# A fused ReLU-gated MLP: the unused branch's DMAs moved to GpSimd, the last pair of output blocks reordered, and its last piece copied out by two engines

## The chip, the cores and the metric

The kernel runs on one core of one Trainium2 chip. The metric is device microseconds (us) of one execution. A timed group of runs lists every execution; most groups here have five or six of the kernel under test and eleven of the kernel before, taken in the same rounds on the same chip. A ratio is the mean time of one kernel's runs over that of the other's in the same rounds, so it is not quite the ratio of the medians that are quoted beside it. (In the experiments the recorded ratios come out, to within 0.0001, when the first run of each kernel, the profiled one, is left out; where means are quoted below, they are of all runs.)

## The reference

```python
def reference(x, w1, w2):                # x 16x256x512, w1 512x4096, w2 2048x512, float32
    h = x @ w1
    gate, value = np.split(h, 2, axis=-1)
    h = np.maximum(gate, 0) * value
    return (h @ w2).astype(np.float32)
```

## The kernel before

The kernel computes both matrix products by a seven-product scheme (products P1 to P7 with precomputed sums of blocks, instead of eight) in 16-bit floats. That is only accurate enough if the data are of ordinary size, so while it works it gathers statistics, and a verdict `unfit` chooses at the end whether a plain "general way" recomputes everything. With these inputs the general way never runs, but all five engines come to that branch at the end of every execution.

```python
    with ExitStack() as fast:
        unfit = fast_way(fast, tc, x2, w1, w2, out2, flag)
    with tc.If(unfit > 0, label="general"):
        with ExitStack() as general:
            general_way(general, tc, x2, w1, w2, out2)     # its DMAs all on nc.sync

# fast_way, second product: a Pair is two 128-row output blocks, made of seven products.
        def P2(self):
            self.o = tmp.tile([P, 2, DO], F32, name="o", tag="tmp")
            nc.scalar.activation(self.o[:, 0, :DO // 2], self.X, COPY, scale=1 / GS)
            if self.end:
                self.send(0, slice(0, DO // 2))            # send: nc.sync.dma_start to the output
        # ... P6 (ScalarE copies Y to pu), P3 and P7 (VectorE: o <- W or Y, + pu; then send) ...
        def P4(self):
            nc.scalar.activation(self.o[:, 1, :DO // 2], self.Y, COPY, scale=1 / GS)
            self.send(1, slice(0, DO // 2 if self.end else DO))

    # order of the products in the last pair (number 3) of the last block of rows:
    LAST_ORDER = ORDER.replace("P5 3, P2 3, P6 3, P3 3, P7 3", "P2 3, P6 3, P5 3, P7 3, P3 3")   # then P4 3
```

TensorE's program is thousands of instructions, fetched while it runs. The kernel starts with 24 warm-up matmuls (`NWARM`) on zeros; some experiments alter those to shift the program by a few instructions.

## Time and profile before

| | before |
|---|---|
| time, median of the first 3 runs | 309.0 us (308.88 to 310.2) |
| span of the profiled execution | 307.5 us |
| TensorE busy, granted clock | 98%, 0.996 |
| last matmul issued, its result ready | 302.66, about 302.93 |
| last store issued by SyncE, landed | 303.38, 305.81 |
| end | 307.46 |

The page of the kernel before; PE is TensorE. The last line is the chain of waits that ended last, by engine.

```profile
span 307.5 us, 5285 instructions
...
PE 300.7 (98%) x1905; PEld 184.0 (60%) x1905; DVE 235.9 (77%) x388; ACT 176.4 (57%) x348; POOL 151.4 (49%) x189
...
PE 96%; DMA 1%; SPq 0%; POOL 0%; ACT 0%; issue 0%
```

TensorE is the bound for 303 us. Nothing in the change touches the number of matmuls, so what is at stake is the tail after 302.93. Its parts are read from the timeline (columns: start us, length us, what) and from the views of single source lines (count: shortest/median/longest ns, first and last start us). First the last copy, and the last store with its time from issue to landing (a store has landed when the semaphore that its shares count up has received the last of them):

```profile
302.97 0.39 ACT L405 ACTIVATE o<-Y 128x256 f32<-128x256 f32 x1 [2.23 <-PE Y L362]
...
L370 SPq DMA_DIRECT2D out_dram<-o x1: 1072/1072/1072, 303.4 to 303.4; - x1
...
DMA to landing us min/median/max: 2.4/2.4/2.4
```

Then the line of the `If` in the kernel before, which each engine's sequencer (marked q) passes, and SyncE's closing waits:

```profile
L42 SPq EVENT_SEMAPHORE  x8: 17/17/17, 305.0 to 305.8; - x8
...
L42 PEldq COMPARE_BRANCH  x1: 496/496/496, 301.8 to 301.8; - x1
L42 DVEq COMPARE_BRANCH  x1: 90/90/90, 302.1 to 302.1; - x1
...
L42 SPq COMPARE_BRANCH  x1: 73/73/73, 304.5 to 304.5; - x1
```

```profile
L785 SPq EVENT_SEMAPHORE  x11: 28/28/28, 305.9 to 306.5; - x11
L785 SPq DRAIN  x2: 7/10/13, 306.6 to 306.6; - x2
```

Two things stand out. SyncE has eight bookkeeping waits on the not-taken side of the `If`; the eighth waits for the last store to land (305.81), and only then come eleven more closing waits: 1.65 us from landing to the end of the span. And the issue of the last store took 1.07 us where 0.33 is usual.

DMA records of that stretch (303 to 306 us) also show queues that carry no data of the kernel, but instructions:

```profile
q1 hardware_dynamic: 298, 0.27, 27.7%
q8 instruction: 1, 0.02, 2.1%
q14 instruction: 2, 0.02, 1.9%
```

### The profile page before, as it was taken

The numbers are of one execution on the slowest core, as the hardware profiler recorded it, in microseconds if no ns is written. First come the engines' busy times: TensorE is split into PE (matmuls) and PEld (weight loads), VectorE is DVE, ScalarE is ACT, GpSimd is POOL, SyncE is SP. The second block draws the span as 40 slices with busy tenths as digits, with TensorE's granted clock in tenths as the row PEclk, the third lists the DMA queues.
The fourth block names the chain that finished last, engine by engine and source line by source line (L and its number), as shares of the span: only waits on it lengthen the run. The fifth ranks groups of instructions, "written<-read, shape, count | busy, mean of one in ns | idle before, by whom it ended". The sixth has DMA issues, their size and how long they took to land.

```text
span 307.5 us, 5285 instructions
## 1 busy us (share of the span) xinstructions
PE 300.7 (98%) x1905; PEld 184.0 (60%) x1905; DVE 235.9 (77%) x388; ACT 176.4 (57%) x348; POOL 151.4 (49%) x189
## 2 busy tenths in 40 slices
PE   7999999999999999999999999999999999999994
PEld 6844444588844444478864444458884444448883
DVE  2579888899768888887438888889536888888841
ACT  2488886455865555538845555546865555553231
POOL 2389999800069899200029889700007998700000
PEclk9999999999999999999999999999999999999998
DMA  6976779964765260001354910000335110001132
GB/s 207 357 257 190 227 177 174 225 123 87 270 193 86 69 136 3 0 0 67 136 175 103 207 34 2 0 2 24 115 108 167 35 34 0 3 1 34 53 120 74
DMA packets 35837, 32.88 MB, mean 107 GB/s; under 512 B 14432, under 2 KB 31328, under 8 KB 35680
## 3 DMA queue, kind: packets, MB, share of 16 engines
q1 hardware_dynamic: 33536, 26.22, 28.0%
q0 software_dynamic: 2272, 6.29, 11.4%
q8 instruction: 16, 0.26, 0.4%
q14 instruction: 13, 0.11, 0.1%
HBM read 27.26 MB, written 12.58 MB: 130 GB/s over the span
## 4 chain that ended last, share of the span: by engine, by line
PE 96%; DMA 1%; SPq 0%; POOL 0%; ACT 0%; issue 0%
PE Y L250 26%; PE X L250 17%; PE W L250 17%; PE Y L362 14%; PE X L362 9%; PE W L362 9%; DMA w_stage<-in_w_dram 1%; PE X L325 1%; PE W L325 1%; PE Y L325 1%; PE Y L498 0%; PE X L498 0%; SPq L488 0%; PE Y L154 0%; POOL w_B L466 0%; ACT o L405 0%
## 5 line engine op out<-in xcount | busy, mean ns | idle before, releaser
L250 PEld LDWEIGHTS <-w_T 128*128 128x128 f16 x496 | 48.3, 98 | 57.3 <-POOL w_T L232 1.1
L179 POOL TENSOR_TENSOR fold<-xh 128x1024 f32<-128x1024 f16 x16 | 30.3, 1894 | 94.5 <-DMA xh<-x 93.7
L250 PE MATMUL X<-x_A,w_B 128*128 128x512 f16 x248 | 73.8, 379 | 0.0
L250 PE MATMUL Y<-x_S,w_T 128*128 128x512 f16 x220 | 65.5, 379 | 0.0
L250 PEld LDWEIGHTS <-w_B 128*128 128x128 f16 x372 | 36.4, 98 | 42.0
L277 DVE SCALAR_TENSOR_TENSOR cc<-W,pu 128x512 f32<-128x512 f32 x62 | 42.9, 691 | 21.2 <-ACT pu L271 20.4
L257 ACT COPY Y<-X 128x512 f32<-128x512 f32 x62 | 35.4, 571 | 38.2 <-PE X L250 37.9
L271 ACT ACTIVATE pu<-Y 128x512 f32<-128x512 f32 x62 | 37.1, 598 | 33.9 <-PE Y L250 32.9
L182 POOL TENSOR_TENSOR fold<-fold 128x512 f32<-128x512 f32 (+2 forms) x96 | 51.8, 539 | 7.5
L362 PEld LDWEIGHTS <-w_stage 128*128 128x128 f16 x512 | 50.0, 98 | 5.8
L287 DVE SCALAR_TENSOR_TENSOR cc<-Y,pu 128x512 f32<-128x512 f32 x62 | 42.9, 691 | 6.7
L282 DVE SCALAR_TENSOR_TENSOR g<-X,cc 128x512 f16<-128x512 f32 x62 | 42.8, 691 | 2.3
L299 DVE SCALAR_TENSOR_TENSOR g<-Y,cc 128x512 f16<-128x512 f32 x62 | 42.2, 681 | 1.8 <-PE Y L250 1.8
L362 PEld LDWEIGHTS <-g 128*128 128x128 f16 x384 | 37.6, 98 | 8.2
L264 ACT ACTIVATE pu<-W 128x512 f32<-128x512 f32 x62 | 37.2, 600 | 0.8 <-PE W L250 0.6
L250 PE MATMUL W<-x_S,w_B 128*128 128x512 f16 x124 | 36.9, 379 | 0.0
L250 PE MATMUL W<-x_S,w_T 128*128 128x512 f16 x124 | 36.9, 379 | 0.0
L250 PE MATMUL Y<-x_A,w_T 128*128 128x512 f16 x124 | 36.9, 379 | 0.0
L362 PE MATMUL X<-w,g 128*128 128x256 f16 x256 | 31.9, 273 | 0.0
L394 DVE SCALAR_TENSOR_TENSOR o<-W,pu 128x256 f32<-128x256 f32 x16 | 6.8, 422 | 19.8 <-PE W L362 19.8
L169 DVE TENSOR_TENSOR w_stage<-g 128x1024 f16<-128x1024 f16 x32 | 21.4, 683 | 0.2
L232 POOL TENSOR_TENSOR w_T<-w_stage 128x512 f16<-128x512 f32 (+1 forms) x16 | 18.7, 1177 | 2.5 <-DMA w_stage<-in_w_dram 2.5
(100 smaller groups left out, 306.2 us busy)
## 6 DMA issues: line engine op xcount, KB each, us to landing
w_stage<-in_w_dram SPq DMA_DIRECT2D x14, 512.0 KB, 6.2
out_dram<-o SPq DMA_DIRECT2D x26, 256.0 KB, 2.1
x<-in_x_dram POOLq DMA_DIRECT2D x4, 1024.0 KB, 9.0
xh<-x SPq DMA_DIRECT2D x16, 256.0 KB, 3.0
w<-in_w_dram POOLq DMA_DIRECT2D x2, 1024.0 KB, 10.2
out_dram<-o SPq DMA_DIRECT2D x12, 128.0 KB, 1.7
w_stage<-in_w_dram SPq DMA_DIRECT2D x4, 256.0 KB, 5.4
x_S<-in_x_dram SPq DMA_DIRECT2D x4, 256.0 KB, 6.1
```

The costliest lines, as they stand in the source:

```text
L169: eng.tensor_tensor(o[n], o[i0], o[i1], op=op)
L179: nc.gpsimd.tensor_tensor(fold, t, t, op=MULT)
L182: nc.gpsimd.tensor_tensor(fold[:, :, :m], fold[:, :, :m], fold[:, :, m:2 * m], op=ADD)
L250: nc.tensor.matmul(ps, wop[wn][:, b, self.jb * P:(self.jb + 1) * P], self.xo[xn][:, b, :], start=fresh and b == 0, stop=b == 1, skip_group ...
L257: nc.scalar.copy(out=self.Y, in_=self.X)
L264: nc.scalar.activation(self.p5, self.W, COPY, scale=GS)
L271: nc.scalar.activation(self.u2, self.Y, COPY, scale=GS)
L277: nc.vector.scalar_tensor_tensor(out=self.c12, in0=self.W, scalar=GS, in1=self.u2, op0=MULT, op1=ADD)
L282: nc.vector.scalar_tensor_tensor(out=self.g[:, self.jb, :TH], in0=self.X, scalar=0.0, in1=self.c12, op0=MAX, op1=MULT)
L287: nc.vector.scalar_tensor_tensor(out=self.c22, in0=self.Y, scalar=GS, in1=self.p5, op0=MULT, op1=ADD)
L299: nc.vector.scalar_tensor_tensor(out=self.g[:, self.jb, TH:], in0=self.Y, scalar=0.0, in1=self.c22, op0=MAX, op1=MULT)
L362: nc.tensor.matmul(ps, self.op[an][:, i], vop[wn][:, i], start=name in ("P1", "P5") and i == 0, stop=i == NJ // 2 - 1, skip_group_check=True)
```

## The change

The intent: take SyncE's bookkeeping off the end by letting GpSimd, idle since 290 us, own the general way's DMAs; let the stores of the last pair leave as early as possible; and halve the last copy by giving it to two engines.

```diff
 # general_way: all four dma_start calls (two for weights, one for x, one for the output)
-            nc.sync.dma_start(...)
+            nc.gpsimd.dma_start(...)
 # class Pair
+        def outputs(self):                     # makes self.o if P2 or P7 is the first to need it
+            if self.o is None:
+                self.o = tmp.tile([P, 2, DO], F32, name="o", tag="tmp")
         def P4(self):
-            nc.scalar.activation(self.o[:, 1, :DO // 2], self.Y, COPY, scale=1 / GS)
+            split = DO // 4 if self.end and self.t == NB // 2 - 1 else DO // 2
+            nc.scalar.activation(self.o[:, 1, :split], self.Y[:, :split], COPY, scale=1 / GS)
+            if split < DO // 2:
+                nc.vector.tensor_scalar(out=self.o[:, 1, split:DO // 2], in0=self.Y[:, split:],
+                                        scalar1=1 / GS, scalar2=None, op0=MULT)
             self.send(1, slice(0, DO // 2 if self.end else DO))
-    LAST_ORDER = ORDER.replace("P5 3, P2 3, P6 3, P3 3, P7 3", "P2 3, P6 3, P5 3, P7 3, P3 3")
+    LAST_ORDER = ORDER.replace("P5 3, P2 3, P6 3, P3 3, P7 3", "P6 3, P5 3, P7 3, P2 3, P3 3")
```

Below, the three parts are called *GpSimd DMAs*, *order* and *split*.

More of the change, by code (lines that the diff above doesn't have):

```diff
@@ L62, in general_way @@
             t = xp.tile([P, 1024], F32, name="g_t", tag="g_t")
-            nc.sync.dma_start(out=t, in_=w1[k * P:(k + 1) * P, j:j + 1024])
+            nc.gpsimd.dma_start(out=t, in_=w1[k * P:(k + 1) * P, j:j + 1024])
             nc.vector.tensor_copy(out=w1_sb[:, k, j:j + 1024], in_=t)
@@ L66, in general_way @@
         t = xp.tile([P, DO], F32, name="g_t", tag="g_t")
-        nc.sync.dma_start(out=t, in_=w2[h * P:(h + 1) * P, :])
+        nc.gpsimd.dma_start(out=t, in_=w2[h * P:(h + 1) * P, :])
         nc.vector.tensor_copy(out=w2_sb[:, h], in_=t)
@@ L72, in general_way @@
             t = xp.tile([P, D], F32, name="g_t", tag="g_t")
-            nc.sync.dma_start(out=t, in_=x2[c * TH + b * P:c * TH + (b + 1) * P, :])
+            nc.gpsimd.dma_start(out=t, in_=x2[c * TH + b * P:c * TH + (b + 1) * P, :])
             for k in range(NK):
@@ L93, in general_way @@
             nc.vector.tensor_copy(out=o, in_=p[:, :DO])
-            nc.sync.dma_start(out=out2[c * TH + b * P:c * TH + (b + 1) * P, :], in_=o)
+            nc.gpsimd.dma_start(out=out2[c * TH + b * P:c * TH + (b + 1) * P, :], in_=o)
 def fast_way(ctx, tc, x2, w1, w2, out2, flag):
@@ L344, in __init__ @@
         def __init__(self, s, g, t):
-            self.s, self.t = s, t
+            self.s, self.t, self.o = s, t, None
             self.end = s == NS - 1 and t != NB // 2 - 2
@@ L382, in P2 @@
         def P2(self):
-            self.o = tmp.tile([P, 2, DO], F32, name="o", tag="tmp")
+            self.outputs()
             nc.scalar.activation(self.o[:, 0, :DO // 2], self.X, COPY, scale=1 / GS)
@@ L398, in P7 @@
         def P7(self):
+            self.outputs()
             nc.vector.scalar_tensor_tensor(out=self.o[:, 1, DO // 2:], in0=self.Y, scalar=1 / GS, in1=self.pu[:, 0],
@@ L404, in P4 @@
         def P4(self):
-            nc.scalar.activation(self.o[:, 1, :DO // 2], self.Y, COPY, scale=1 / GS)
+            split = DO // 4 if self.end and self.t == NB // 2 - 1 else DO // 2
+            nc.scalar.activation(self.o[:, 1, :split], self.Y[:, :split], COPY, scale=1 / GS)
+            if split < DO // 2:
+                nc.vector.tensor_scalar(out=self.o[:, 1, split:DO // 2], in0=self.Y[:, split:], scalar1=1 / GS, scalar2=None,
+                                        op0=MULT)
             self.send(1, slice(0, DO // 2 if self.end else DO))
```

## The prediction

> **What bounds the kernel.** The page shows PE busy 98% of 307.5 us, and the chain of waits is 96% PE at a granted clock of 0.996. None of the three edits adds or removes a matmul; the instruction order shows the same 1905 on PE. So only the 4.5 us after the last matmul can change. From the timeline and the per-line views of the last 6 us, that tail runs as follows:
>
> - The last product (P4) starts at 301.89 and its result is ready at about 302.93. ScalarE copies 128x256 from 302.97 for 0.385 us.
> - SyncE issues the last store at 303.38. This issue took 1.07 us where 0.33 is usual. It overlaps a 16 KB fetch of instructions by DMA, 303.06 to 304.07.
> - SyncE's branch is at 304.50, its next instruction at 305.03. There stand eight bookkeeping waits of the `If` (305.03 to 305.83), one per hardware DMA queue semaphore, each of which adds what the general way would have counted. The eighth is passed at 305.83, just after the last store lands (305.81, 2.4 us after its issue).
> - Then 11 closing waits, about 0.062 us each, reach the closing drains at 306.58 and 306.65; 0.81 us of barrier ends at 307.46.
>
> **1. General way's DMAs on GpSimd.** They never run. But the not-taken side of the `If` no longer adjusts the hardware DMA semaphores on SyncE: its eight waits go. GpSimd adjusts the software DMA semaphores instead, at about 289.7, where it branches and then idles to the end. SyncE goes through 12 closing waits, of which the one for the last store is the last. So the other eleven (11 x 0.062 = 0.68 us) run while the store is landing, instead of after it. From landing to the drain: now 0.77 us, then about 0.1. Saves about 0.65 us, all on the critical path. SyncE's jump over the general way's instructions also shortens (ScalarE's, over none, took 0.13 us where SyncE's took 0.46); the Trainium skill ("Runtime: NRT & Kernel Launch", Instruction fetch mechanics) says that a taken branch to a page not held forces a fetch. I expect this to be hidden behind the landing.
>
> **2. Last copy split.** The built program makes VectorE wait for ScalarE's half, not for PE. The Trainium skill ("PSUM — Partial Sum Buffer", PSUM bank collisions raise a hardware error) says two engines must not touch one bank at once, so the halves run in series. Estimates from widths 256 and 512 in this trace: ScalarE 0.28 us, VectorE 0.29, handover 0.05: the store is ready at 303.61 instead of 303.36, 0.25 us later. This loses, unless it hides in the issue's stall: if that still ends near 304.45, landing stays at 305.8; without the stall it lands near 305.5.
>
> **3. Order P6 P5 P7 P2 P3 P4.** P3 and P4 stay last. P7's store leaves 0.87 us earlier, P2's later; neither ends the kernel. P6's operands are ready 0.26 us before it starts. Zero.
>
> **Sum.** 0 (order), 0 to +0.25 (split), -0.65 (waits), 0 to -0.3 (stall or branch): about -0.7 us. Predicted 308.3 us, 8 in 10 within 307.8 to 308.9. Faster by over 2%: 0.01; within: 0.98; slower: 0.01.
>
> **What would show it.** On SyncE, no waits of the `If` line after its branch, 12 closing waits, the last passed at the landing, and the drain about 0.1 us later. VectorE's 128x128 copy starts after ScalarE's ends. PE's end is unchanged at 302.9.
>
> **What would make it wrong.** PE stalling in the new order; the last issue stalled longer, or not at all; SyncE reaching the last wait only after the landing; GpSimd's software-DMA bookkeeping holding it up beyond 305; a run-to-run spread (308.9 to 310.2) as large as the gain.

## The result

309.04 us median (308.64 to 309.22, 6 runs) against 309.47 (308.88 to 310.2, 6 runs): ratio 0.9986, 95% interval 0.9971 to 1.0001. That is within 2%, as forecast, but outside the predicted range of 307.8 to 308.9; the gain is 0.4 us and not 0.7. A second group gave 308.77 against 309.38, ratio 0.9989 (0.9976 to 1.0003).

The profile after, in the same order. The page:

```profile
span 307.4 us, 5284 instructions
...
PE 300.7 (98%) x1905; PEld 184.8 (60%) x1905; DVE 236.9 (77%) x389; ACT 176.2 (57%) x348; POOL 151.2 (49%) x189
```

The last copy, now in two halves, and the last store:

```profile
302.85 0.28 ACT L411 ACTIVATE o<-Y 128x128 f32<-128x128 f32 x1 [1.36 <-PE Y L362]
...
303.15 0.29 DVE L413 TENSOR_SCALAR o<-Y 128x128 f32<-128x128 f32 x1 [0.76 <-ACT o L411]
...
L374 SPq DMA_DIRECT2D out_dram<-o x1: 332/332/332, 303.5 to 303.5; - x1
...
DMA to landing us min/median/max: 3.0/3.0/3.0
```

The line of the `If`, and SyncE's closing waits:

```profile
L42 POOLq EVENT_SEMAPHORE  x5: 17/43/43, 289.8 to 290.2; - x5
...
L42 PEldq COMPARE_BRANCH  x1: 1976/1976/1976, 300.8 to 300.8; - x1
...
L42 DVEq COMPARE_BRANCH  x1: 90/90/90, 303.2 to 303.2; - x1
...
L42 SPq COMPARE_BRANCH  x1: 68/68/68, 303.9 to 303.9; - x1
```

```profile
L794 SPq EVENT_SEMAPHORE  x12: 28/28/28, 304.1 to 306.5; - x12
L794 SPq DRAIN  x2: 7/10/13, 306.6 to 306.6; - x2
```

And the DMA records from 303 to 306.5 us (packets, MB, share of 16 engines' time):

```profile
q1 hardware_dynamic: 288, 0.26, 22.7%
q8 instruction: 1, 0.02, 2.6%
q14 instruction: 1, 0.01, 1.2%
```

The first step of the prediction is there to the letter: SyncE's eight waits at the `If` are gone, GpSimd does the bookkeeping at 290, ten of the twelve closing waits are over by 304.7. Landing to end is now 0.96 us (306.47 to 307.43) instead of 1.65. But SyncE then stands at the last two waits for 1.8 us, because the stores had not landed: the last one 3.0 us after its issue instead of 2.4, and the one before it 3.7 us instead of 2.7. What the bookkeeping gave, the landing took back. And TensorE's branch took 1.98 us where it had taken 0.50.

So the question is what holds up stores of 128 KB that could land in 1.7 us (the store just before these two did, in both kernels).

### The profile page after: what moved, and what is told of

The parts are those of the page before. It is cut to its first block, busy times and chain, and to the rows that moved or that the text cites. A ratio compares the mean times of both kernels' runs of the same rounds, so it can differ in the third digit from the quotient of the medians.

```text
span 307.4 us, 5284 instructions
## 1 busy us (share of the span) xinstructions
PE 300.7 (98%) x1905; PEld 184.8 (60%) x1905; DVE 236.9 (77%) x389; ACT 176.2 (57%) x348; POOL 151.2 (49%) x189
## 4 chain that ended last, share of the span: by engine, by line
PE 96%; DMA 2%; SPq 0%; POOL 0%; issue 0%; DVE 0%; ACT 0%
PE Y L250 26%; PE X L250 17%; PE W L250 17%; PE Y L362 14%; PE X L362 9%; PE W L362 9%; DMA w_stage<-in_w_dram 2%; PE X L325 1%; PE W L325 1%; PE Y L325 1%; PE Y L507 0%; SPq L497 0%; PE X L507 0%; PE Y L154 0%; POOL w_B L475 0%
```

## The theories and the experiments

**Theory A: fetches of instructions.** The q8 records are TensorE's program: each is 16,384 bytes, and from the fifth to the thirteenth, eight fetches, TensorE starts 2,048 instructions in the kernel before, 256 for each fetch. (That q8 is TensorE's is inferred from this count.) One such fetch begins 0.7 to 1.4 us after the end of TensorE's branch in every trace that has the branch. A store is cut into 16 shares (its semaphore is updated 16 times), taken here as one for each DMA engine; a fetch is one record of 0.9 to 1.5 us, taken to lie on one engine. The share of the store that queues behind it should come late, and a store has landed only when its last share has.

The semaphore records of the trace show each share. In the changed kernel, 15 shares of the store before last had landed by 304.12 and the sixteenth at 306.16. Later runs are added here to see whether it is a rule; all times are us in the trace, from the records of instruction packets and semaphore updates:

```
kernel                    TensorE's 16 KB     store before last:        last store:
                          fetch, to           15th share, 16th share    16th share
before                    303.06  304.07      305.04  305.25            305.81 (its issue stalled)
changed                   303.53  304.97      304.12  306.16            306.47
changed, again            303.14  304.34      303.69  305.51            305.82
GpSimd DMAs alone         303.51  304.43      305.00  305.62            305.93
GpSimd DMAs + order       304.13  305.29      305.09  306.48            306.79
GpSimd DMAs + split       302.96  304.39      304.16  305.58            306.14 (its issue stalled)
```

In all six, the sixteenth share of the store before last lands 1.17 to 1.19 us after the end of the fetch, and the last store 0.31 us after that (or, where its issue stalled, 1.74 to 1.75 us after the fetch). Where the fifteenth share is late as well (305.00 to 305.09 in three rows), it comes 0.95 to 1.13 us after the end of an 8 KB fetch on queue 14, of which more below. The Trainium skill ("DMA: Bandwidth & Descriptors", Queues, rings and completion order) says that a DMA engine serves its queues in turn, a packet at a time, and, in its section Why a DMA increments its semaphore by 16 and not by 1, that a DMA's semaphore counts its shares. Both fit. The DMA packet records of GpSimd DMAs + order show the wait itself: after 305.2 only 18 packets of stores are left, one after another. The first starts at 305.27, as the fetch ends (305.29). Eight of 1 KB and one of 4 bytes are the late share of the store before last; the next nine, to 306.34, are the last store's. No record here names the engine, so that it is the same one is still inferred.

**Theory B: the change's own later and closer stores.** The split makes the last store later and the order moves the others; the landing follows. **Chance:** landings of stores scatter.

The first group: one part alone, the split undone, TensorE's branch later, and no branch at all.

**GpSimd DMAs alone** (the changed kernel with the other two parts undone).

```diff
-            split = DO // 4 if self.end and self.t == NB // 2 - 1 else DO // 2
+            split = DO // 2
-    ... "P6 3, P5 3, P7 3, P2 3, P3 3")
+    ... "P2 3, P6 3, P5 3, P7 3, P3 3")
```

> The general way's DMAs on GpSimd alone; old order of the last pair, last piece copied by ScalarE alone. Theory A (the bookkeeping is gone as predicted, but what ends the kernel is the landing of the last two stores, held up by a 16 KB fetch of instructions that falls among them): the drain follows the last landing by about 0.08 us (0.77 before); the last store is issued at 303.3 to 303.4; its landing takes 2.3 to 3.0 us if a 16 KB fetch lies within 1 us of its issue; span 306.6 to 307.2, time 0.2 to 0.7 us under the kernel before. Theory B (the split and the order delay the landing): without them the landing is as in the kernel before, about 2.4 us after the issue at 303.38, so 305.8, span 306.75, time 0.7 us under the kernel before.

Measured: 308.61 us against 309.07, ratio 0.9969 (0.9947 to 0.9992). In the trace the last store, issued at 303.26, landed at 305.93, 2.67 us later; span 306.9. So by the ratios part of the change alone gains more than the whole: 0.31% of 309, nearly 1 us (the intervals overlap; the second group repeats it). The landing is late here too, as A has it, but B's 2.4 us is not far off: this run alone does not separate the two.

**GpSimd DMAs and order, no split.**

```diff
-            split = DO // 4 if self.end and self.t == NB // 2 - 1 else DO // 2
+            split = DO // 2
```

> The changed kernel with its last piece copied by ScalarE alone. Theory A: the last store is issued 0.20 to 0.25 us earlier than in the changed kernel (303.25 instead of 303.47), but the landing still ends with the share of the DMA engine that also fetched instructions, near 306.0 to 306.5; time within 0.3 us of the changed kernel. Theory B (the split costs its 0.25 us in full): landing and time 0.25 us earlier.

Measured: 309.03 against 309.07, ratio 0.9984 (0.9966 to 1.0002), as slow as the changed kernel. Relative to TensorE the store left earlier, but its landing is tied to the fetch (table above). TensorE's branch took 1.94 us. This run differs from the one before by the order alone (means 309.01 and 308.49, not clear of the noise). The 0.25 us that B expected from undoing the split does not show.

**TensorE's branch later, by 8 idle matmuls.**

```diff
             advance(stream, 112, jobs)
+            late = new_w()
+            for _ in range(8):
+                arm(late)          # 512 columns of zeros into a spare buffer
```

> The changed kernel with 8 idle matmuls of 512 columns (8 x 0.216 = 1.7 us) at the end of TensorE's program, so that TensorE branches 1.7 us later and nothing else moves. Theory A: the 16 KB fetch that began at 303.53 begins at about 305.2, after the last store's data has gone; the last two stores land 1.7 to 2.0 us after their issue (all 16 shares by about 305.4); span about 306.4, time 0.8 to 1.1 us under the changed kernel. Theory B, and the theory that the late landing is chance: landing unchanged near 306.2 to 306.5, time unchanged or later.

Measured: 309.04 against 309.07, ratio 0.9991. A miss: the fetch did not move as expected. It began at 304.01, not 305.2, because the branch is taken by the sequencer, which runs well ahead of the matmuls: it came to the branch at 301.77, with all eight idle matmuls and the eight of P4 still to be issued. Still, the store before last now escaped (landed in 1.87 us) and the late share, 306.12, was the last store's, 1.18 us after the end of the fetch (304.94).

**No branch: the `If` and its general way left out** (right for these inputs only).

```diff
-    with tc.If(unfit > 0, label="general"):
-        with ExitStack() as general:
-            general_way(general, tc, x2, w1, w2, out2)
```

> The changed kernel without the If and its general way (right for these inputs; the verdict is computed and loaded but not used): no engine branches at the end. Theory A: no 16 KB fetch within the last 3 us; the last two stores land 1.7 to 2.0 us after their issue; span 306.2 to 306.5, time 0.8 to 1.2 us under the changed kernel. Theory B and chance: landing near 306.2 to 306.5 as in the changed kernel, time within 0.3 us of it.

Measured: 307.86 against 309.07, ratio 0.995 (0.9931 to 0.9968). The last store, and the fetches of the whole execution from the page of this run (16 on q8 in the kernel before and the changed one):

```profile
L371 SPq DMA_DIRECT2D out_dram<-o x1: 332/332/332, 303.5 to 303.5; - x1
...
DMA to landing us min/median/max: 1.7/1.7/1.7
```

```profile
q8 instruction: 15, 0.25, 0.4%
```

Split and order are as in the changed kernel, the store is issued at the same 303.48, and it lands at 305.18 instead of 306.47. B, which would leave the landing where it was, falls as the main cause: it is the branches and what they fetch. All engines' branches went here, so this run does not say whose.

The second group repeats the changed kernel and GpSimd DMAs alone on another chip, adds the remaining pair of parts, and tries again to hold TensorE's branch back, now with many small matmuls.

**The changed kernel again.**

> The changed kernel itself once more, as the standard of this group and to see whether its tail repeats. Theory A (stores held up by the fetches after the branches; a wait of TensorE's branch for the page fetched before it): TensorE's branch again takes about 2 us (0.4 to 0.5 with the old order), its 16 KB fetch ends about 304.9, the store before last lands 1.19 us after that end and the last one another 0.31 us later. Chance: other landings, with no such spacing.

Measured: 308.77 against 309.38, ratio 0.9989. Branch 2.04 us, fetch's end 304.34, landings 1.17 and 1.48 us after it: the tail repeats.

**GpSimd DMAs alone, again.**

> The general way's DMAs on GpSimd alone, once more, on one chip with the changed kernel. Theory A: TensorE's branch takes 0.4 to 0.5 us, its fetch ends about 304.4 and the last store lands 1.5 us later, near 305.9; time 0.3 to 0.6 us under the changed kernel, so the order and the split together cost that. Chance: the same time as the changed kernel within 0.15 us.

Measured: 308.3 against 309.38, ratio 0.9969 (0.9956 to 0.9982), branch 0.50 us. In this trace the whole execution ran 0.7 us later and the last store's issue stalled (0.99 us), so the landing was 1.74 us after the fetch's end. On this chip it is 0.43 us under the changed kernel (means 308.44 and 308.87; 95% of such a difference lies within about 0.5 us, so it is not clear of the noise by itself).

**GpSimd DMAs and split, old order.**

```diff
-    ... "P6 3, P5 3, P7 3, P2 3, P3 3")
+    ... "P2 3, P6 3, P5 3, P7 3, P3 3")
```

> The changed kernel with the old order P2 P6 P5 P7 P3 P4, so DMAs on GpSimd and the split. Theory A, order part: with the old order the TensorE fetch before the branch starts near 298.4 instead of 299.9, the branch takes 0.4 to 0.5 us instead of 2, the fetch after it ends about 304.1 to 304.5; the last landing comes 1.5 us after the later of that end and, for one share, follows VectorE's own 8 KB fetch, which the split moves from 303.5 to 304.4 or later: near 306.0; time 0.2 to 0.5 us under the changed kernel. Rival (the split is what costs, not the order): as slow as the changed kernel.

Measured: 308.56 against 309.38, ratio 0.9977 (0.9964 to 0.999); branch 0.50 us. With the old order the branch took 0.41 to 0.50 us in all four traces so far, with the new one 1.3 to 2.0 us in all four.

**TensorE's branch held back by 44 tiny matmuls** (GpSimd DMAs, old order, no split).

```diff
             advance(stream, 112, jobs)
+            late = new_w()
+            for _ in range(44):
+                nc.tensor.matmul(late[:32, :64], warm_b[:, :32], warm_b[:, :64], start=True, stop=True)
```

> DMAs on GpSimd alone, and 44 tiny matmuls (32 columns of weights, 64 of data) at the end of TensorE's program, so that its sequencer, which runs some 32 instructions ahead, reaches the branch late. Theory A: the branch comes near 304 and its fetch starts after 304.7, when the last store's data has gone: the last store lands 1.7 to 2.0 us after its issue at 303.27, near 305.1 to 305.3; span 306.1 to 306.3, time 0.5 us or more under DMAs on GpSimd alone and the fastest that keeps the general way. If the tiny matmuls take over 0.055 us each, TensorE itself ends after 305.3 and takes part of it back. Chance: no change.

Measured: 308.01 against 309.38, ratio 0.9964 (0.9949 to 0.9979). Its branch, and the landing of its last store:

```profile
L42 PEldq COMPARE_BRANCH  x1: 412/412/412, 303.4 to 303.4; - x1
```

```profile
L374 SPq DMA_DIRECT2D out_dram<-o x1: 332/332/332, 303.1 to 303.1; - x1
...
DMA to landing us min/median/max: 2.0/2.0/2.0
```

The branch came at 303.40, the fetch began at 304.56, and the last store landed 2.0 us after its issue, at 305.13. The tiny matmuls took 0.03 us each and TensorE was done at 304.1, before anyone waited for it. It keeps the general way, and it is faster than both kernels. It is 0.34 us under GpSimd DMAs alone (means 308.10 and 308.44), where 0.5 or more was expected, and that is within the noise. By the spacing, what is left of the delay belongs to the 8 KB fetch on queue 14 (303.36 to 303.68): the store before last landed at 304.83, 1.15 us after its end, and the last one 0.3 us later.

### Why the new order makes the branch long

The built program shows which semaphores TensorE waits for, instruction by instruction. P7 must wait until ScalarE has copied P6's result. In the new order P7 is the third of the last six products, not the fourth, so this wait stands 16 instructions earlier. **Theory D:** the sequencer runs ahead until a wait that is not met. In the old order it ran past the end of a 16 KB page of program before it met that wait, and the next page was asked for early (298.37 in the kernel before). In the new order the wait stands just before the end of the page: the fetch began at 299.90, after ScalarE's copy was done (298.86). TensorE's branch then has to wait for this fetch: in the six traces with the long branch (two of the changed kernel, two of GpSimd DMAs + order, the 8 idle matmuls, and the converse below) it ended 1.44 to 1.46 us after the end of that fetch. And the fetch that follows the branch is later in turn: it began 0.55 to 1.58 us after the start of the last matmul in these six traces, and 0.39 to 0.97 in the four with the old order and its short branch. **Rival E:** the order as such crowds the stores.

The test moves the end of the page without touching the last pair: more or fewer instructions in the warm-up.

**Changed kernel, page's end 20 instructions earlier.**

```diff
-    for i in range(NWARM):
+    for i in range(NWARM - 3):
         nc.tensor.matmul(Y[:, :P], warm_b[:, :P], warm_b[:, :P], start=True, stop=True)
+    for i in range(13):
+        nc.tensor.matmul(Y[:32, :64], warm_b[:, :32], warm_b[:, :64], start=True, stop=True)
```

> The changed kernel with 20 more instructions in TensorE's warm-up (3 of its 24 matmuls replaced by 13 tiny ones, about the same time), so that the point at which the sequencer asks for its next 16 KB of program comes 20 instructions earlier in the last pair: before the wait of P7 for the copy of P6 instead of just after it. Theory D (the new order costs because that wait holds the sequencer short of the page's end, the page comes 1.5 us late and the branch has to wait for it): the fetch before the branch starts near 298.4 instead of 299.9, the branch takes 0.4 to 0.5 us instead of 2 and ends near 301.3, the fetch after it ends at 303.0 to 304.1; VectorE's fetch still falls on the last store; last landing 305.2 to 306.0, time 0.3 to 1.0 us under the changed kernel (308.8). Rival E (the order itself moves the stores together, whatever the pages): branch still 2 us, no gain.

Measured: 309.4 against 309.08, ratio 1.0011 (0.9998 to 1.0024). The branch was short, as D says; the time, expected 0.3 to 1.0 us shorter, went the other way. The fetch, now 302.53 to 303.85, fell on the issue of the store before last, which stalled for 1.33 us; the last store had to wait for SyncE until 304.31; and then VectorE's own fetch (below) fell on both of their shares, and the last landed at 307.01.

**The same without the split.**

```diff
-            split = DO // 4 if self.end and self.t == NB // 2 - 1 else DO // 2
+            split = DO // 2
```

> The same, without the split: DMAs on GpSimd, new order, the page's end before the wait. Theory D: as the one before, and VectorE's fetch starts near 303.5 and ends 303.8: last landing 304.95 to 305.4, span 305.9 to 306.4, time 0.8 to 1.2 us under the kernel with the same order and no split (309.0): the new order is then better than the old, not worse. Rival E: 309.0 as before.

Measured: 308.35 against 309.08, ratio 0.9981 (0.9963 to 0.9999), last landing 305.21. 1.1 us under the run with the split on the same chip (means 308.33 and 309.43). The kernel with the same order, no split and the page's end after the wait had 309.03 in another group: 0.7 us by the medians, where 0.8 to 1.2 was expected. That the new order would then be better than the old does not show (0.9981 against 0.9969 twice).

**The converse: old order, page's end 16 instructions later** (GpSimd DMAs, no split).

```diff
-    for i in range(NWARM):
-        nc.tensor.matmul(Y[:, :P], warm_b[:, :P], warm_b[:, :P], start=True, stop=True)
+    for i in range(NWARM - 8):
+        nc.tensor.matmul(Y[:, :192], warm_b[:, :P], warm_b[:, :192], start=True, stop=True)
```

> The converse: DMAs on GpSimd, old order, no split, and 16 instructions fewer in TensorE's warm-up (16 matmuls of 192 columns for 24 of 128), so that the page's end falls after the same wait in the old order. Theory D: the fetch before the branch starts at 300.6 to 301.2 instead of 298.4, the branch takes 1.4 to 2 us instead of 0.45, the fetch after it ends at 305.0 to 305.8, last landing 306.5 to 307.3, time 0.6 to 1.2 us over the same kernel with the page as it was (308.4). Rival E: 308.4, branch 0.45 us.

Measured: 309.34 against 309.08, ratio 1.0015 (1.0002 to 1.0028), where the same kernel with 24 warm-up matmuls has 0.9969 twice. The branch lines of these three runs, in that order:

```profile
L42 PEldq COMPARE_BRANCH  x1: 496/496/496, 301.3 to 301.3; - x1
```

```profile
L42 PEldq COMPARE_BRANCH  x1: 496/496/496, 300.8 to 300.8; - x1
```

```profile
L42 PEldq COMPARE_BRANCH  x1: 1716/1716/1716, 301.2 to 301.2; - x1
```

The new order with a short branch, the old order with a long one: it is not the order but where the page ends. D stands and E falls for the branch. The other traces agree: where the branch is long, the fetch before it began 0.96 to 1.66 us after the end of the copy of P6's result, and where it is short, before that end (by 0.03 to 1.49 us), except in the two runs below that hold a new-order branch back until the fetch is long over. The last landing of the converse came 3.29 us after its issue.

**The branch held back, again** (the kernel with 44 tiny matmuls).

> The version with TensorE's branch held back by 44 tiny matmuls, once more beside these. All theories that the fetch delays the landing: 308.0 to 308.2, last landing 1.7 to 2.1 us after its issue.

Measured: 307.93 against 309.08, ratio 0.9967 (0.9954 to 0.998); landing 2.03 us after the issue.

### What the order and the split cost by themselves

Four more runs, on one chip, because the sizes were open: the order with TensorE's fetch out of the way, the split likewise, and the two page positions side by side.

**GpSimd DMAs, new order, no split, TensorE held back** (the 44 tiny matmuls added to the run without the split).

> DMAs on GpSimd, new order, no split, TensorE's branch held back by 44 tiny matmuls. Theory D (the order costs only through TensorE's fetch): as with the old order held back: branch 0.4 to 0.5 us at 303.4, last store issued near 303.2 and landing 1.7 to 2.1 us later, time 0.9 to 1.2 us under the kernel before. Rival E (the order itself bunches the stores): 0.3 to 0.5 us slower than that.

Measured: 307.51 us (307.28 to 307.97) against 309.39, ratio 0.9935 (0.9919 to 0.9951): the fastest version that keeps the general way, 1.9 us under the kernel before by the medians (0.9 to 1.2 was expected). Its branch and last store:

```profile
L42 PEldq COMPARE_BRANCH  x1: 412/412/412, 303.7 to 303.7; - x1
```

```profile
L374 SPq DMA_DIRECT2D out_dram<-o x1: 332/332/332, 303.5 to 303.5; - x1
...
DMA to landing us min/median/max: 1.8/1.8/1.8
```

With the fetch out of the way the new order costs nothing that shows. (It had 0.9935, the old order held back 0.9964 and 0.9967, but on other chips; that the new order is better is not claimed.)

**The changed kernel, TensorE held back** (the 44 tiny matmuls added to the changed kernel; this differs from the last run by the split alone).

> The changed kernel with TensorE's branch held back. If the split costs by its later store alone: 0.2 us over the run without the split. If it costs by VectorE's fetch as well, which begins 1.2 us after VectorE's branch, so near 304.3: one share of the last store lands 1.1 us after that fetch's end, near 305.7 to 306.3, and the time is 0.5 to 0.9 us over the run without the split.

Measured: 309.06 against 309.39, ratio 0.9986 (0.9969 to 1.0002). The split alone costs 1.35 us here (means 308.92 and 307.57; 1.6 us by the ratios), more than either expectation. So in the changed kernel holding TensorE's branch back gains nothing that the times show: 0.9986 with it, 0.9986 and 0.9989 without. The later store is 0.22 us of it (below). VectorE's fetch accounts for some more: an 8 KB fetch on queue 14 begins 1.19 to 1.21 us after the start of VectorE's branch in all traces with the new order (1.20 to 1.58 with the old; that it is VectorE's is inferred from this), and the split puts that branch after VectorE's half of the last copy. In this trace the fetch was 304.21 to 304.87, beginning 0.9 us after the last store's issue, and the last share came at 305.67. That trace was the fastest of its group (span 306.6; the other four 306.8 to 307.4), so the rest of the 1.35 us is not seen in it.

**GpSimd DMAs and order, again, and the same with the page's end before the wait**, side by side.

> DMAs on GpSimd and new order, no split, page's end after the wait: TensorE's branch about 2 us, last landing 1.5 us after its fetch's end; 0.3 to 0.6 us under the kernel before.

> The same with the page's end before the wait: branch 0.5 us, last landing by 305.5; Theory D: 0.3 us or more under the run with the page's end after the wait. If the fetch, now earlier, holds up the issue of the last stores as often as it held their landing, the two take the same time.

Measured: 309.21 (ratio 1.0001, 0.9982 to 1.002) with the page's end after the wait, 308.56 (0.9971, 0.9955 to 0.9987) with it before: 0.73 us between the means. The first was slower than expected; its branch took 1.54 us and its last store landed 1.50 us after the fetch's end. In the second the branch took 0.50 us and the fetch, 301.90 to 303.12, was early enough for the landing (305.35) but stalled the issue of the store before last for 1.23 us. Early is better than late, and out of the way is best.

To compare the traces, which start their last product at times that differ by over a microsecond, take the time from the start of the last matmul of P4 to the last landing:

| kernel | TensorE's branch, us | last matmul to last landing, us | time over before |
|---|---|---|---|
| before | 0.50 | 3.15 | 1 |
| changed (two groups) | 1.98, 2.04 | 3.93, 3.72 | 0.9986, 0.9989 |
| changed, 8 idle matmuls | 1.32 | 3.39 | 0.9991 |
| changed, page's end before the wait | 0.50 | 4.01 | 1.0011 |
| changed, branch held back | 0.41 | 3.28 | 0.9986 |
| GpSimd DMAs alone (two groups) | 0.41, 0.50 | 3.39, 3.08 | 0.9969, 0.9969 |
| GpSimd DMAs + order (two groups) | 1.94, 1.54 | 3.94, 3.56 | 0.9984, 1.0001 |
| GpSimd DMAs + split | 0.50 | 3.57 | 0.9977 |
| GpSimd DMAs, page's end after the wait | 1.72 | 4.01 | 1.0015 |
| GpSimd DMAs + order, page's end before the wait (two groups) | 0.50, 0.50 | 2.66, 2.98 | 0.9981, 0.9971 |
| GpSimd DMAs, branch held back (two groups) | 0.41, 0.41 | 2.72, 2.75 | 0.9964, 0.9967 |
| GpSimd DMAs + order, branch held back | 0.41 | 2.49 | 0.9935 |
| changed without the `If` | none | 2.64 | 0.995 |

From the landing to the end of the span it is 1.65 us in the kernel before and 0.96 in all others.

Each entry of the third column is one execution, so it follows the times only roughly: a trace can be of the fastest run of its group (GpSimd DMAs + order, again: 307.86 of 307.86 to 310.59). With five or six runs each, the difference of two versions' means is uncertain by 0.4 to 0.9 us (95%, estimated from the spread of the runs). Clear of that are the split's 1.1 and 1.35 us, and on one chip the converse over the old order held back, 1.38 us (means 309.34 and 307.96). The 0.43 and 0.73 us above are not clear of it by themselves.

## Why the prediction was wrong, point by point

- **What bounds the kernel, and the tail's parts: right.** TensorE's end did not suffer (last matmul started at 302.66 before, 302.54 after).
- **Step 1, the bookkeeping: right in mechanism and size.** Predicted 0.65 us off the way from landing to end; measured 1.65 to 0.96, so 0.69 us. SyncE's jump shortened from 0.46 us to 0.14 and was hidden, as forecast. Alone, this part gained 0.31% twice, nearly 1 us; the intervals (0.2 to 1.6 and 0.6 to 1.4 us) include 0.69.
- **Step 2, the split: half right.** The halves ran in series: ScalarE's ended at 303.12, VectorE's began at 303.15. That fits the bank rule of the Trainium skill ("PSUM — Partial Sum Buffer", PSUM bank collisions raise a hardware error), turned into a wait by the built program; that the wait is there for this rule is inferred. From the start of the last matmul to the issue of the store it took 0.72 us before and 0.94 after, so 0.22 us later, where 0.25 was predicted. What failed is the sentence "if that still ends near 304.45, landing stays at 305.8; without the stall it lands near 305.5". There was no stall, and it landed at 306.47. A store that is issued before the fetch need not escape it: here one of its shares was still behind the fetch. I had tied the landing to the issue; it is tied to the fetch.
- **Step 3, the order: "Zero" was wrong.** The dataflow argument (who is ready when, which store is last) held, and with TensorE's branch held back the order costs nothing that shows. But it moved a wait across the end of a page of TensorE's program, which lengthened the branch from 0.5 to 2 us and made the fetch after it later. By the ratios, order and split together took back more than half of what GpSimd DMAs alone gain (0.31% alone, 0.11 to 0.14% with all three).
- **The sum.** Predicted -0.65 (waits) and 0 to +0.25 (split), with the landing where it was or earlier. In the two traces: -0.69 from landing to end, +0.78 from the last matmul to the landing, of which 0.22 is the later store and the rest, by the records of the shares, the fetches. These nearly cancel in the profiled pair; over all runs 0.3 to 0.4 us of the gain remained by the ratios.
- Among what would make it wrong the prediction lists "the last issue stalled longer, or not at all". It looked at the issue of the store, and the cost sat in the landing.

What stays open: that the late share and the fetch are on the same DMA engine is inferred, no record names it; and of the 1.35 us that the split costs with TensorE held back, one trace shows only a part. So how the changed kernel's loss divides between TensorE's fetch and VectorE's is open: holding TensorE's back alone did not recover it, leaving out all branches did. The general way itself ran in no execution here, on either queue.

## What to carry to other kernels

An engine's branch at the end of a program is not free even where it is not waited for: here a fetch of program followed each of TensorE's branches, one share of the last stores had to wait for its end, and a store has landed only when its slowest share has. When a tail is worth tuning, list the instruction fetches beside the stores and try to hold the branch of the engine with the large program until the stores' data has gone. Here 44 idle matmuls of 0.03 us did that where the split was left out (0.9964, 0.9967 and 0.9935); with the split, which makes VectorE branch late too, they gained nothing (0.9986). And judge each part of a change by itself: this one held a gain of 0.3% and two parts that, by the ratios, together hid more than half of it.

## What the Trainium skill lacked or had wrong

- "Runtime: NRT & Kernel Launch", Instruction fetch mechanics, calls the fetch of the next block "mostly hidden". It does not say that the fetch delays data: a store's share landed 1.17 to 1.19 us after the fetch's end in the six traces of the first table, and the last store took 2.4 to 3.3 us from issue to landing in the ten traces where TensorE's fetch began between 0.6 us before its issue and 0.9 us after, against 1.7 without a branch.
- The same section says that a taken branch to a page not held must fetch it "before execution can continue". The costly 16 KB fetch is of another kind: in the kernel before it began at 303.06, after TensorE had executed its first instruction behind the branch (302.97), so TensorE did not wait for it. (Whether the branch's target was held no record shows, so this does not contradict the page.) Nor does the section say that a branch waits for the fetch asked for before it: it ended 1.44 to 1.46 us after that fetch in six traces, and took 1.3 to 2.0 us instead of 0.4 to 0.5.
- The same section gives 16 KiB blocks. The q8 fetches are that (16,384 bytes, 256 instructions); those on queue 14, one of which follows VectorE's branch, are 8,192 bytes.
- "Perfetto Trace Analysis", DMA Instruction — HWDGE (DVE, Sync), explains the length of an issue by a lock and the making of descriptors, and does not name a fetch of instructions as what can prolong it: SyncE's issue of the last store while a fetch was on took 0.99 to 1.27 us instead of 0.33, and ended 0.37 to 0.38 us after the fetch (kernel before, GpSimd DMAs alone again, GpSimd DMAs and split). Not every such issue stalls: in the changed kernel one at 300.75, 0.85 us into a fetch, took 0.33. What decides is not shown.
- No page says that the place where the sequencer stops at an unmet wait decides when the next page of program is asked for: 298.37 in the kernel before, 299.90 in the changed one. TensorE's came to its branch with 16 matmuls still to be issued (8 idle matmuls).
